# New cost figures for the planner that orders background work in a hybrid conv/SSM decoder step

## The chip, the cores and the metric

One NeuronCore of a Trainium2 chip. The time is device microseconds (us) of one execution, as the median of several; lower is better.

## What is computed

One layer for 2048 prompt tokens and 8 single-token samples, in fp32: a convolution branch and a state-space (SSM) branch from one input projection, each gated, an output projection, and a per-layer embedding step. Cut to what matters:

```python
h = rmsnorm(x, g_pre)
proj = h @ w_in                       # 1024 -> 6144 columns
u = c_a * sigmoid(c_b)
v, new_buf = causal_depthwise_conv(u, conv_buf, conv_w, conv_b)   # 31 taps
v = silu(layernorm(v, ln_g, ln_b)) * silu(c_z)
y_c = v @ w_pc
ys, sr, si = ssm_branch(s_x, ...)     # 32 groups, 64 complex states
ys = gelu(ys)
ys = ys * sigmoid(ys @ w_glu + b_glu) * silu(s_z)
y_s = ys @ w_ps
m = sigmoid(gc) * y_c + sigmoid(gs) * y_s
x = x + rmsnorm(m @ w_out, g_post)
e = rmsnorm(p @ w_ple, g_ple)
x = x + e * sigmoid(x @ w_pg + b_pg)
```

## The kernel before

**Tiles.** Channels lie on the 128 partitions, tokens along the free axis. The tokens are worked through in two halves: half 0 is 1024 prompt tokens and the 8 samples (blocks of 344 columns, three to a tile), half 1 the other 1024 (two blocks of 512). An fp32 product is made of three fp32r products on TensorE (PE): weight high part by activation high part (L288), high by low (L289), low by high (L290). ScalarE (ACT) makes the high part of a weight chunk, `whi` (L251), and GpSimd (POOL) the low part, `wlo` (L331, from `w_split`); there are four buffers of each. Activations have a high and a low part in the same way (`hh`/`hl`, `nh`/`nl`, `mh`/`ml`); the low part is a subtraction on VectorE (DVE) or POOL.

**Foreground.** `stages()` takes one weight chunk, issues for each block 3·k matmuls into one of the PSUM banks, adds their cost to the planner's PE clock (L293), lets the planner place background work (`bg.pump()`), and then writes the instruction that takes the result out of the bank. `stage_pair` (cost at L310) does the same for two chunks at once.

**Background.** Everything else is a task of the class `Background`: a Python generator that yields (engine, time from which it may run) and then writes one or a few instructions. `pump` compares the planner's own clocks of DVE (V), ACT (S) and POOL (G) with its PE clock and writes a task's next step into the program when it would start before PE's present time. So nothing is scheduled on the chip: the planner's costs `cV`, `cS`, `cG`, `cP4` (L138 to L142) and the PE cost decide where in each engine's in-order stream a step stands. `pick` (L90) decides between DVE and POOL for a subtraction or an addition. `drain` writes a task's remaining steps at once when the foreground needs them, and `room(n)` holds a task until n SBUF units are free.

The tasks that are named below:
- `ssm_setup`: a chain of small DVE operations on `spar` and `ph` tiles that ends in the tiles `gw` and `gt`; the first use by PE is a transpose of `gt` (L609).
- `rms_task`: sums of squares, `rt` on ACT (L984) and `re<-re,rt` on DVE.
- `conv_task`: the 31 taps of one channel tile, each one DVE operation `acc<-u,prm,acc` (L183). If enough units are free, `conv_side` takes two of the taps at a time from the other end with ACT (`cq`, L881) and POOL (`ca`), and `u<-acc,ca` joins the two sums on DVE.
- `ln_task` and `mean_task`: the layer norm of the conv output. The two means over the channels are PE products with a constant matrix (`nh` and `nl` by `avgr`, L363 and L364), each followed by ACT and DVE work. The first is called the mean product here, the second the norm product; each occurs once in either half.
- `gelu_task` (L1151) and `ysn_task` (L1206): the SSM output's activation and its split. `x1_task`: the residual after `w_out` (`o`, `xr`, then `mh` and `ml`). `y_task`: the last step (`e`, `sgp`).

A DVE step that evacuates or multiplies out a PSUM bank (`gs<-bank,gs`, `u<-bank,sg`) stands in the same in-order stream as the taps.

Of the kernel before, what the change touches and what calls it, by code (L numbers as in the profile page):

```python
# [21 lines left out]
G = 32  # L22
# [5 lines left out]
class Background:  # L28
# [61 lines left out]
    def pick(self, n, ready):  # L90

        v, g = (max(self.clock[e], ready) for e in "VG")
        return "V" if v + n / 960.0 <= g + n / 478.0 + 0.3 else "G"

    def use(self, e, cost, ready=0.0):

# [11 lines left out]
class Units:  # L108
# [8 lines left out]
    def alloc(self, dtype=F32, shape=None, name="un"):  # L117
        assert self.free_list, "no unit is free: " + " ".join(sorted(t.name for _, t in self.slot.values()))
        i = self.free_list.popleft()
        self.least = min(self.least, len(self.free_list))  # L120
        t = self.pool.tile([P, UW], dtype, tag=f"u{i}", name=f"{name}_{i}")
        self.slot[id(t)] = (i, t)
        return t
# [4 lines left out]
    def free(self, *ts):  # L128
        for t in ts:
            i, _ = self.slot.pop(id(t))  # L130
            self.free_list.append(i)


def build(nc, tc, A, O):
    V, S, T, GP, SY = nc.vector, nc.scalar, nc.tensor, nc.gpsimd, nc.sync
    bg = Background()
    use, fore = bg.use, bg.fore
    cV = lambda n: 0.08 + n / 960.0  # L138
    cV2 = lambda n: 0.08 + n / 1920.0
    cS = lambda n: 0.13 + n / 1250.0  # L140
    cG = lambda n: 0.16 + n / 478.0
    cP4 = lambda n: 4 * max(n, 128) / 2400.0  # L142
    queue = {"issue": 0.0, "data": 0.0}

# [13 lines left out]
    with ExitStack() as ctx:  # L158
# [12 lines left out]
        def bank():  # L171
            return ps_pool.tile([P, 512], F32, tag="bank", name="bank")
# [17 lines left out]
        def room(k):  # L190
            while units.left() < k:
                yield None, bg.now + 0.5
# [88 lines left out]
        def stages(key, todo):  # L281
            wt, k = take(key)
            for i, (m, rhs, evac, c0, n) in enumerate(todo):
                w = slice(m * P, m * P + P)
                o = bank()[:, 0:n]
                for kt in range(k):
                    (hi, lo), (rh, rl) = wt[kt], rhs[kt]
                    T.matmul(o, hi[:, w], rh[:, c0:c0 + n], start=kt == 0, stop=False)  # L288
                    T.matmul(o, hi[:, w], rl[:, c0:c0 + n], start=False, stop=False)  # L289
                    T.matmul(o, lo[:, w], rh[:, c0:c0 + n], start=False, stop=kt == k - 1)  # L290
                if i == 4 and wstate["split"] == wstate["use"]:
                    w_ahead(wstate["use"] - 1)
                bg.pe += 3 * k * (n / 2400.0 + 0.003)  # L293
                bg.pump()
                evac(m, o, c0, n)

        def stage_pair(keys, rhs, blocks, evacs):

            wts = [take(key, 0)[0] for key in keys]
            pts = [[bank()[:, 0:n] for _, n in blocks] for _ in keys]  # L300
            for kt, (rh, rl) in enumerate(rhs):
                e = kt == len(rhs) - 1
                for wt, os_ in zip(wts, pts):
                    hi, lo = wt[kt]
                    for o, (c0, n) in zip(os_, blocks):
                        T.matmul(o, hi, rh[:, c0:c0 + n], start=kt == 0, stop=False)
                        T.matmul(o, hi, rl[:, c0:c0 + n], start=False, stop=False)
                        T.matmul(o, lo, rh[:, c0:c0 + n], start=False, stop=e)  # L308
            w_ahead(wstate["use"], 0)
            bg.pe += 6 * len(rhs) * sum(n / 2400.0 + 0.003 for _, n in blocks)  # L310
            bg.pump(pe=False)
            for os_, evac in zip(pts, evacs):
                for o, (c0, n) in zip(os_, blocks):
                    evac(0, o, c0, n)
# [29 lines left out]
        def hilo(name):  # L344
            return alloc(F32R, name=name + "h"), alloc(F32R, name=name + "l")
# [733 lines left out]
        def half(h, hT, finish):  # L1079
            n, blocks = TOK[h], BLOCKS[h]  # L1080
# [68 lines left out]
            zs, ysg = [None] * NB, [None] * NB  # L1149

            def gelu_task(b):  # L1151
                yield "S", ready[b]
                zs[b] = alloc(name="z")
                S.activation(out=zs[b][:, 0:HT].rearrange("p (s q) -> p q s", q=8),
                             in_=ysb[b][:, 0:HT].rearrange("p (q s) -> p q s", q=8), func=AF.Gelu_apprx_tanh)
                if h == 0:
                    S.activation(out=zs[b][:, HT:n], in_=ysb[b][:, HT:n], func=AF.Gelu_apprx_tanh)
                free(ysb[b])
                r = use("S", cS(n) + 1.4, ready[b])
                yield from room(2)  # L1160
                ysg[b] = hilo("y")
                yield from split_task(zs[b], ysg[b], full, "G", r)
# [41 lines left out]
            free(sgl)  # L1204

            def ysn_task(b):  # L1206
                yield "S", ready[b]
                ysn[b] = hilo("yn")
                yield from split_task(zs[b], ysn[b], full, "A", ready[b])
                free(zs[b])  # L1210
# [375 lines left out]
```

## Time and profile before

| | |
|---|---|
| runs | 1972.57, 1973.45, 1979.47 us; median 1973.45 |
| profiled execution | 1971.99 us, span of its instructions 1970.2 us |
| PE busy | 1918.5 us (97%), 10386 matmuls |
| DVE busy | 1442.1 us (73%), 1696 instructions |
| ACT busy | 765.6 us (39%), 1276 instructions |
| POOL busy | 784.8 us (40%), 573 instructions |
| mean granted PE clock | 0.989 of full |

A share of busy time is a mean over the whole program. PE's busy time counts a matmul from its start to its modelled end, so matmuls that follow each other overlap; how fast PE goes is read from how many start in a stretch. A number in square brackets behind a row of a timeline is the time in which the engine stood idle before it, with what ended that time.

### The profile page before, as it was taken

What the parts mean: (1) busy time and instruction counts of PE and PEld (TensorE: products, weight loads), DVE (VectorE), ACT (ScalarE), POOL (GpSimd) and SP (SyncE); (2) the same over time, 40 slices, a digit from 0 to 9 for tenths busy, and PEclk for the clock granted to TensorE, in tenths of its full rate; (3) what the DMA queues carried; (4) which work ended last, traced back from release to release, by engine and by line L of the source; (5) the groups of instructions that cost most, each with busy time, mean ns of one, the idle gap of its engine ahead of it and who ended that gap; (6) DMA issues with size and microseconds to landing.
All of it is one profiled execution on the core that took longest, in us unless ns stands there. A gap on an engine that the chain in (4) does not pass through costs nothing.

```text
span 1970.2 us, 26641 instructions
## 1 busy us (share of the span) xinstructions
PE 1918.5 (97%) x10386; PEld 1723.0 (87%) x10386; DVE 1442.1 (73%) x1696; ACT 765.6 (39%) x1276; POOL 784.8 (40%) x573
## 2 busy tenths in 40 slices
PE   8897999999999999999899999999999999999998
PEld 7797999999999999999798788888888888888877
DVE  6889997899899876444884479888589843442686
ACT  7424211227311364254532223444731353223542
POOL 1437623315422223253533222687743222224554
PEclk9998999999999999999899999999999999999999
DMA  8461344542122215342554463212212211422455
GB/s 315 155 203 62 100 133 141 177 144 78 51 83 78 102 50 193 116 142 93 190 197 164 172 200 123 74 60 91 71 48 75 97 67 43 160 107 77 148 189 174
DMA packets 103286, 243.58 MB, mean 124 GB/s; under 512 B 11752, under 2 KB 44648, under 8 KB 103144
## 3 DMA queue, kind: packets, MB, share of 16 engines
q1 hardware_dynamic: 102840, 241.68, 36.2%
q8 instruction: 81, 1.33, 0.3%
q14 instruction: 45, 0.37, 0.1%
q10 hardware_dynamic: 320, 0.20, 0.0%
HBM read 188.17 MB, written 54.62 MB: 123 GB/s over the span
## 4 chain that ended last, share of the span: by engine, by line
PE 85%; issue 4%; DVE 4%; POOL 2%; ACT 1%; DMA 1%; POOLq 0%; ACTq 0%; SPq 0%; DVEq 0%
PE bank L288 27%; PE bank L290 26%; PE bank L289 26%; PE bank L774 2%; POOL wlo L331 1%; PE bank L777 1%; PE bank L719 1%; DMA raw<-in_w 1%; POOL ca L331 1%; DVE sgp L331 1%; DVE o L183 0%; DVE o L331 0%; DVE ml L331 0%; DVE spar L183 0%; PE bank L308 0%
## 5 line engine op out<-in xcount | busy, mean ns | idle before, releaser
L331 POOL TENSOR_TENSOR wlo<-raw,whi 128x512 fp32r<-128x512 f32 x386 | 566.5, 1486 | 1082.2 <-ACT whi L251 1064.5
L288 PE MATMUL bank<-hh,whi 128*128 128x344 f32 (+1 forms) x1888 | 665.9, 353 | 0.9 <-ACT whi L251 0.9
L289 PE MATMUL bank<-hl,whi 128*128 128x344 f32 (+1 forms) x1888 | 659.9, 350 | 6.8 <-DVE hl L331 6.8
L290 PE MATMUL bank<-hh,wlo 128*128 128x344 f32 (+1 forms) x1888 | 661.2, 350 | 1.4 <-POOL wlo L331 1.4
L183 DVE SCALAR_TENSOR_TENSOR acc<-u,prm,acc 128x1024 f32<-128x1024 f32 x412 | 530.5, 1288 | 11.2
L289 PEld LDWEIGHTS bank<-hl,whi 128*128 128x128 f32 x1888 | 356.9, 189 | 39.4 <-DVE hl L331 7.1
L288 PEld LDWEIGHTS bank<-hh,whi 128*128 128x128 f32 x1888 | 356.4, 189 | 36.9 <-ACT whi L251 1.5
L290 PEld LDWEIGHTS bank<-hh,wlo 128*128 128x128 f32 x1888 | 356.8, 189 | 35.6 <-POOL wlo L331 2.4
L251 ACT CAST whi<-raw 128x512 fp32r<-128x512 f32 x388 | 223.9, 619 | 148.5 <-PE bank L289 68.6
L288 PE MATMUL bank<-mh,whi 128*128 128x344 f32 (+1 forms) x640 | 227.4, 355 | 7.7 <-ACT whi L251 5.8
L290 PE MATMUL bank<-mh,wlo 128*128 128x344 f32 (+1 forms) x640 | 227.1, 355 | 5.2 <-POOL wlo L331 5.1
L289 PE MATMUL bank<-ml,whi 128*128 128x344 f32 (+1 forms) x640 | 226.6, 354 | 0.3 <-DVE ml L331 0.3
L331 POOL TENSOR_TENSOR ca<-ca,cq 128x512 f32<-128x512 f32 x104 | 132.2, 1300 | 39.5 <-ACT cq L881 36.1
L288 PEld LDWEIGHTS bank<-mh,whi 128*128 128x128 f32 x640 | 122.6, 192 | 20.8 <-ACT whi L251 7.1
L290 PEld LDWEIGHTS bank<-mh,wlo 128*128 128x128 f32 x640 | 122.7, 192 | 18.9 <-POOL wlo L331 7.8
L289 PEld LDWEIGHTS bank<-ml,whi 128*128 128x128 f32 x640 | 122.5, 191 | 12.3 <-DVE ml L331 1.1
L289 PE MATMUL bank<-vl,whi 128*128 128x344 f32 (+1 forms) x320 | 111.9, 350 | 0.7 <-DVE vl L331 0.7
L288 PE MATMUL bank<-vh,whi 128*128 128x344 f32 (+1 forms) x320 | 112.2, 351 | 0.0
L290 PE MATMUL bank<-vh,wlo 128*128 128x344 f32 (+1 forms) x320 | 112.0, 350 | 0.0
L881 ACT ACTIVATE cq<-u,prm 128x512 f32<-128x512 f32 x104 | 73.4, 722 | 55.0 <-POOL ca L331 45.9
L331 DVE TENSOR_TENSOR oacc<-oacc,sq 128x344 f32<-128x344 f32 (+1 forms) x35 | 30.6, 874 | 79.2 <-ACT sq L1388 78.7
L177 DVE TENSOR_TENSOR gcl<-bank,gcl 128x344 f32<-128x344 f32 (+1 forms) x40 | 23.5, 587 | 65.7 <-PE bank L290 65.7
(213 smaller groups left out, 2447.7 us busy)
## 6 DMA issues: line engine op xcount, KB each, us to landing
raw<-in_w SPq DMA_DIRECT2D x194, 512.0 KB
cq<-cq SPq DMA_DIRECT2D x12, 512.0 KB
e<-e SPq DMA_DIRECT2D x8, 516.0 KB
rt<-e SPq DMA_DIRECT2D x8, 516.0 KB
gc<-gc SPq DMA_DIRECT2D x8, 516.0 KB
m<-gs SPq DMA_DIRECT2D x8, 516.0 KB
gcl<-gc SPq DMA_DIRECT2D x8, 516.0 KB
m2l<-m SPq DMA_DIRECT2D x8, 516.0 KB
```

The lines of the kernel that those rows point to most:

```text
L177: V.tensor_tensor(out=out, in0=a, in1=b, op=op)
L183: V.scalar_tensor_tensor(out=out, in0=a, scalar=s, in1=b, op0=op0, op1=op1)
L251: S.copy(out=hi, in_=t[:, c])
L288: T.matmul(o, hi[:, w], rh[:, c0:c0 + n], start=kt == 0, stop=False)
L289: T.matmul(o, hi[:, w], rl[:, c0:c0 + n], start=False, stop=False)
L290: T.matmul(o, lo[:, w], rh[:, c0:c0 + n], start=False, stop=kt == k - 1)
L331: (V if e == "V" else GP).tensor_tensor(out=out, in0=a, in1=b, op=op)
L719: T.matmul(pvs[rr][half_[i], jj], we[:, g * P + rr * 64:g * P + rr * 64 + 64], U[:, g, 8:8 + ne], start=True, stop=True)
L774: T.matmul(pvs[i][:, jj], TW[:, :, 2 * j + i], U[:, 2 * j + i, o0:136], start=True, stop=False)
L777: T.matmul(pvs[i][:, jj], cq[half_[i], x * 512 + j * P:x * 512 + (j + 1) * P], X[half_[i], x, j, o0:136], start=False, stop=x == 1)
L881: S.activation(out=q[:, h], in_=u[:, k + x * 512:k + x * 512 + 512], func=AF.Identity, scale=w(k))
```

## The change

The planner's costs are replaced by other numbers, with a function of its own for a product (`cPr`), and two tasks wait for free SBUF units before and after their first yield.

```diff
     def pick(self, n, ready):
         v, g = (max(self.clock[e], ready) for e in "VG")
-        return "V" if v + n / 960.0 <= g + n / 478.0 + 0.3 else "G"
+        return "V" if v + n / 930.0 <= g + n / 478.0 + 0.4 else "G"
...
-    cV = lambda n: 0.08 + n / 960.0
+    cV = lambda n: 0.1 + n / 930.0
     cV2 = lambda n: 0.08 + n / 1920.0
-    cS = lambda n: 0.13 + n / 1250.0
-    cG = lambda n: 0.16 + n / 478.0
+    cS = lambda n: 0.13 + n / 1190.0
+    cG = lambda n: 0.3 + n / 478.0
+    cPr = lambda n: 0.007 + n * 0.4375e-3
...
-                bg.pe += 3 * k * (n / 2400.0 + 0.003)
+                bg.pe += 3 * k * cPr(n)
...
-            bg.pe += 6 * len(rhs) * sum(n / 2400.0 + 0.003 for _, n in blocks)
+            bg.pe += 6 * len(rhs) * sum(cPr(n) for _, n in blocks)
...
             def gelu_task(b):
+                yield from room(1)
                 yield "S", ready[b]
+                yield from room(1)
...
             def ysn_task(b):
+                yield from room(2)
                 yield "S", ready[b]
+                yield from room(2)
```

The work is the same; its order on the engines is not. The instructions of PE are the same in number, those of the background products stand elsewhere among the others. DVE has 410 instead of 412 taps `acc<-u,prm,acc`, and one `hl<-xT,hh` more, which POOL had. ACT has 44 instead of 38 table loads, and 108 instead of 104 `cq`; POOL 108 instead of 104 `ca`.

**DVE up to the mean product of half 0.** `u_3341` and `u_3323` are the last channel tile of the convolution, `gs<-bank,gs` takes a result of `w_ps` out of PSUM, and `nl` is the low part that the mean product needs. Before:

```order
L177 TENSOR_TENSOR gs_6114<-bank,gs_6114 128x344
L183 SCALAR_TENSOR_TENSOR acc<-u_3341,prm,acc 128x1024 x5
L183 SCALAR_TENSOR_TENSOR u_3341<-u_3341,prm,acc 128x1024
L1271 COPY u_3341<-vsm 128x8
L331 TENSOR_TENSOR acc_5266<-u_3341,acc_5266 128x1032
L331 TENSOR_TENSOR nl_6512<-acc_5266,nh_6511 128x1032
```

Now:

```order
L178 TENSOR_TENSOR gs_5822<-bank,gs_5822 128x344
L184 SCALAR_TENSOR_TENSOR acc<-u_3323,prm,acc 128x1024 x12
L184 SCALAR_TENSOR_TENSOR u_3323<-u_3323,prm,acc 128x1024
L1276 COPY u_3323<-vsm 128x8
L332 TENSOR_TENSOR acc_5276<-u_3323,acc_5276 128x1032
L332 TENSOR_TENSOR nl_6295<-acc_5276,nh_6294 128x1032
L178 TENSOR_TENSOR gs_6128<-bank,gs_6128 128x344 x2
```

The six evacuations `gs_6113` and `gs_6114` of before, now `gs_6128` and `gs_6129`, have moved behind `nl`. On PE the mean product stands 180 matmuls earlier. At the last evacuation ahead of these six (`gs_5809` before, `gs_5822` now) DVE has 207 taps behind it, where it had 192.

**DVE in the SSM setup.** `bb`, `spar` and `rho` are the setup's chain, `re<-re,rt` is a step of a norm that waits for `rt` of ACT. Before:

```order
L177 TENSOR_TENSOR bb_729<-bb_729 128x256
L331 TENSOR_TENSOR re_743<-re_743,rt_989 128x1032
L331 TENSOR_TENSOR re_743<-re_743,rt_1102 128x1032
L177 TENSOR_TENSOR spar_727<-spar_727 128x16 x2
L177 TENSOR_TENSOR rho<-spar_727 128x16
```

Now:

```order
L178 TENSOR_TENSOR bb_732<-bb_732 128x256
L332 TENSOR_TENSOR re_741<-re_741,rt_1026 128x1032
L178 TENSOR_TENSOR spar_730<-spar_730 128x16 x2
L178 TENSOR_TENSOR rho<-spar_730 128x16
L560 COPY spar_730<-spar_730 128x16
```

The second of the two norm steps has moved behind the next 25 rows of the chain; on ACT its `rt`, and the one ahead of it, have moved behind a pair of `whi`. Further on, a norm step that stood ahead of the first `gt` has moved behind it, and two taps have moved ahead of it.

**ACT behind the norm product of half 1.** `mean` and `acc` are the end of the norm, `u<-u,prm` its activation on the channel tiles, `gs` the evacuation of a gate with another activation function. Before:

```order
L383 ACT_TABLE_LOAD
L383 ACTIVATE mean_13883<-mean_13882 128x1024
L384 ACTIVATE acc_13159<-mean_13883 128x1024
L322 ACT_TABLE_LOAD
L322 ACTIVATE gs_13766<-bank 128x512
L251 CAST whi<-raw 128x512 x2
L1248 ACT_TABLE_LOAD
L1248 ACTIVATE u_10431<-u_10431,prm 128x1024
L1248 ACTIVATE u_10642<-u_10642,prm 128x1024
```

Now:

```order
L323 ACT_TABLE_LOAD
L323 ACTIVATE gs_13588<-bank 128x512
L252 CAST whi<-raw 128x512 x2
L1253 ACT_TABLE_LOAD
L1253 ACTIVATE u_10431<-u_10431,prm 128x1024
L323 ACT_TABLE_LOAD
L323 ACTIVATE gs_13589<-bank 128x512
L1253 ACT_TABLE_LOAD
L1253 ACTIVATE u_10642<-u_10642,prm 128x1024
```

The norm product has moved 192 matmuls ahead on PE, so its activations now alternate with gate evacuations, each change of function with a table load.

## Rows read from the trace of the kernel before

**Rows 1.** The page's chain of work that ended last: shares of the span.

```profile
PE 85%; issue 4%; DVE 4%; POOL 2%; ACT 1%; DMA 1%; POOLq 0%; ACTq 0%; SPq 0%; DVEq 0%
```

**Rows 2.** Windows: us, busy (x starts) of PE, PEld, DVE, ACT, POOL; clock; DMA.

```profile
500.00:550.00 50.00, 50.00 (x319) 50.00 (x318) 43.28 (x47) 19.93 (x34) 20.66 (x13) 1.00 0.16 45
1500.00:1600.00 100.00, 100.00 (x432) 80.96 (x431) 76.93 (x69) 36.37 (x50) 25.45 (x18) 1.00 0.23 78
```

**Rows 3.** Waits of PE over the span: us in total, times, longest.

```profile
PE bank L609 <- issue: 14.1, 1, 14.1
...
PE bank L289 <- DVE hl L331: 6.8, 1, 6.8
...
PE bank L289 <- DVE psl L331: 0.2, 1, 0.2
```

**Rows 4.** Timeline of PE behind the first transposes of gt: start, us, instruction.

```profile
196.91 0.64 PE L288 MATMUL bank<-hh,whi 128*128 128x344 f32 x1
...
202.07 0.31 PE L288 MATMUL bank<-hh,whi 128*128 128x344 f32 x1
```

**Rows 5.** Timelines of DVE and ACT in the SSM setup.

```profile
104.06 1.23 DVE L331 TENSOR_TENSOR re<-re,rt 128x1032 f32<-128x1032 f32 x1 [5.18 <-ACT rt L984]
...
99.22 1.15 ACT L251 CAST whi<-raw 128x512 fp32r<-128x512 f32 x2
```

**Rows 6.** Timelines of DVE and POOL ahead of the last hl.

```profile
72.69 6.85 DVE L183 SCALAR_TENSOR_TENSOR spar<-spar 128x16 f32<-128x16 f32 x6
...
81.54 1.22 DVE L183 SCALAR_TENSOR_TENSOR spar<-spar 128x16 f32<-128x16 f32 x6
...
83.17 0.87 DVE L331 TENSOR_TENSOR hl<-xT,hh 128x688 fp32r<-128x688 f32 x1
...
75.37 1.70 POOL L331 TENSOR_TENSOR hl<-xT,hh 128x688 fp32r<-128x688 f32 x1
```

**Rows 7.** Costliest groups: one tap; us busy, mean ns of one.

```profile
L183 DVE SCALAR_TENSOR_TENSOR acc<-u,prm,acc 128x1024 f32<-128x1024 f32 x412 | 530.5, 1288 | 11.2
```

**Rows 8.** Waits of DVE from 196 to 626 us, first and last of ten.

```profile
DVE u L177 <- PE bank L290: 10.4, 6, 3.0
...
DVE gs L177 <- PE bank L290: 4.8, 9, 1.6
...
DVE gs L177 <- issue: 0.2, 1, 0.2
```

**Rows 9.** Timelines of DVE and PE at the layer norm of half 0.

```profile
626.25 14.52 DVE L183 SCALAR_TENSOR_TENSOR acc<-u,prm,acc 128x1024 f32<-128x1024 f32 x11
...
672.82 2.21 DVE L331 TENSOR_TENSOR nl<-acc,nh 128x1032 fp32r<-128x1032 f32 x1 [4.05 <-ACT nh L338]
...
704.17 1.23 DVE L331 TENSOR_TENSOR nl<-acc,nh 128x1032 fp32r<-128x1032 f32 x1 [1.12 <-ACT nh L338]
...
677.76 0.32 PE L363 MATMUL bank<-nh,avgr 128*128 128x344 f32 x1
```

**Rows 10.** The stage w_pg of half 0: a window, and DVE's timeline in it.

```profile
936.00:990.00 54.00, 43.17 (x224) 39.79 (x224) 43.61 (x42) 26.97 (x43) 29.15 (x18) 0.85 0.57 194
...
974.16 1.60 DVE L331 TENSOR_TENSOR sgp<-sgp,e 128x344 f32<-128x344 f32 x1
975.79 0.52 DVE L331 TENSOR_TENSOR sgp<-sgp,o 128x344 f32<-128x344 f32 x1
```

**Rows 11.** Timeline of DVE in half 1, up to the mean product.

```profile
1434.41 1.22 DVE L177 TENSOR_TENSOR u<-acc,ca 128x1024 f32<-128x1024 f32 x1 [27.86 <-POOL ca L331]
...
1547.21 1.23 DVE L331 TENSOR_TENSOR nl<-acc,nh 128x1024 fp32r<-128x1024 f32 x1 [1.11 <-ACT nh L338]
```

**Rows 12.** Timelines of PE and ACT at the norm product of half 1.

```profile
1552.45 0.39 PE L363 MATMUL bank<-nh,avgr 128*128 128x512 f32 x1
...
1588.75 1.28 ACT L383 ACT_TABLE_LOAD   x1
1590.04 1.07 ACT L383 ACTIVATE mean<-mean 128x1024 f32<-128x1024 f32 x1
```

## Prediction, made before the changed kernel ran

> **What bounds the kernel now.** I read the chain of waits first: 85% of the span is PE, and no other engine has more than 4% [rows 1]. PE's pace comes next, from the windows: undisturbed it starts 319 matmuls of 344 columns in 50 us, 157 ns each, and 432 of 512 columns in 100 us, 231.5 ns each, at full clock [rows 2]. The planner used to reckon 146 and 216 ns (n/2400 + 0.003); now it reckons 157.5 and 231. So the new product cost is what the rows show. But the planner's clock runs nothing on the chip. It only sets the order, and the order matters only where PE waits. Third, therefore, PE's own waits: eleven kinds, the longest 14.1 us at the first transpose of `gt`, then 6.8 us for `hl` of DVE, the last 0.2 us [rows 3]. What a wait costs beyond itself is in PE's timeline behind the 14.1 us: from 196.91 to 202.07 there are 18 matmul steps, 287 ns each where full clock gives 157, so 18 x 0.13 = 2.3 us more at the lower clock level [rows 4]. The third lossy place is the stage `w_pg` of half 0: in 54 us only 224 matmuls start, which at 157 ns are 35.2 us; 18.8 us are lost at a granted clock of 0.85 [rows 10]. These three places lose about 14.1 + 2.3 + 6.8 + 18.8 = 42 us of 1972. A gain has to come from there. Everywhere else the change can only keep PE fed or stop feeding it.
>
> **The change part by part.** The matmuls are the same, so each part is a question whether its DVE, ACT or POOL step is late for PE.
>
> *The last `hl` of the input norm (PE waits 6.8 us for it).* It still stands behind the same chain of small `spar` operations. One more `hl` goes through DVE (0.87 us) and none through POOL (1.70 us) [rows 6]. The same six small operations took 6.85 us beside POOL and 1.22 us without [rows 6]. If the chain gets faster by the POOL operation's whole length, the wait changes by 0.87 - 1.70 = -0.8; if not at all, by +0.9. I take 0.
>
> *`gt` (PE waits 14.1 us).* The row names no engine, but `gt` is the end of DVE's setup chain, and PE starts as soon as it is there; so what is added to this chain is added to PE's wait. DVE idled 5.18 us for `rt` until 104.06 [rows 5]. Now only the first of the two norm steps stands there, and its `rt` follows the `whi` pair that ends at 99.22 + 1.15 = 100.4 [rows 5]; with about 1.1 us for itself it is done at 101.6, and the norm step at 102.8, against 105.3: -2.5. The second step comes later (+1.2), a later one leaves for behind `gt` (-1.2), two taps come in (2 x 1.29 = +2.6 [rows 7]). The sum is +0.1. Against it, the chain's small operations now run where the old wait lay, beside POOL; six at the price of rows 6 (1.14 instead of 0.20 us) would be +5.6, none would be 0. I take +1, nearer to none since only some 3 us of the old wait are refilled; bounds -2 and +5.
>
> *The mean product of half 0.* This is the largest term that is open. The product stands 180 matmuls earlier: 677.76 - 180 x 0.157 = 649.5 [rows 2, 9]. Its `nl` ended at 672.82 + 2.21 = 675.0 [rows 9]. After the last `gs` evacuation before it, behind which the next taps started at 626.25, DVE now has 12 taps (15.8 us at 14.52/11 = 1.32 [rows 9]), the last tap and two joins (2.9), the wait for `nh` (about 1.2) and `nl` (2.2): 22.1 us, so 648.4 if DVE has no backlog at 626.25. That is 1 us to spare. The backlog is the question: up to that evacuation 15 more taps are placed than before, two of them ahead of `gt`, where PE waits along with DVE. The other 13 are 13 x 1.32 = 17.2 us. Up to 626 us DVE's ten kinds of waits sum to 30.8 us, 10.4 + 4.8 = 15.2 of them for PE's banks [rows 8]; there the stream had nothing else to do, and these the earlier taps fill. 17.2 - 15.2 leaves 2 us, less the 1 to spare: +1. Bounds 0 (all absorbed) and 17.2 - 1 = 16 (none).
>
> *The norm product of half 0* stands 186 matmuls behind the mean product instead of 198: 29.2 us. From the mean product to the end of `nl` the chain took 704.17 + 1.23 - 677.76 = 27.6 us [rows 9]. Six evacuations now lie in it, a norm step has left. Each evacuation adds about 0.6, the step was 2.3, so 28.9 against 29.2, with the matmul itself to finish first: +1, bounds 0 and +3.
>
> *`w_pg` of half 0* is a chain on DVE (43.6 of 54 us busy [rows 10]). Before its last `ml`, now five pairs of `sgp` operations stand instead of four, two operations more of 0.52 to 1.60 us [rows 10]; that is +1.0 to +3.2, I take +2. The `mh` of ACT stand in another order among the `whi`; what that gives I bound by a third of the 18.8 us lost, 6, in favour.
>
> *Half 1.* The mean product moves 168 matmuls ahead: 1552.45 - 168 x 0.2315 = 1513.6 [rows 2, 12]. `nl` ended at 1548.4, 35 us later [rows 11]. What pays for it: the 27.86 us that DVE waited for POOL's `ca` until 1434.4 [rows 11] now hold taps of another tile, four evacuations of 0.6 leave, and one tile has two taps fewer on DVE; 27.9 + 2.4 + 2.6 = 32.9, and a start of the last tile without backlog gives the rest. I take 0, bounds 0 and +4. The four `cq` and `ca` more lie on ACT and POOL, which have room.
>
> *Six more table loads* stand behind half 1's norm product, now among gate evacuations. One takes 1.28 us, and the operation behind it starts 10 ns after it ends (1588.75 + 1.28, then 1590.04) [rows 12]. From the norm product to the weight chunk after next PE has 120 matmuls, 27.8 us [rows 2]. ACT's stream has in it six loads (7.7 us) and 15 operations, by my estimate 12 us; with the wait for DVE's first `u` and POOL's `wlo` behind, some 25 us. So 0, with 3 us of room.
> A rule of the Trainium skill speaks against this part: "ScalarE: Activation LUTs", section "What ACT_TABLE_LOAD costs", states 1283 ns for a load and about 1380 ns of drain with each switch. The first agrees with the row, the second does not: no gap of that size stands behind this load. By the page six switches would be 8.3 us longer, PE would wait some 5 us, and the sum would be 1982; by the row it stays.
>
> The remaining moves (small SSM products by 3 to 18 us, the norm of x by 77 us, earlier) come where DVE has slack; I cost them at nothing. If that cover were gone, each is bounded by one tap ahead of it, 1.3 us.
>
> Sum: 0 + 1 + 1 + 1 + 2 + 0 + 0 = +5 on the profiled execution's 1971.99, thus **1977.0**. The median of the runs is 1973.45, 1.5 above the profiled one; against it the forecast is +3.5. About 0.5%, 9.9 us, is what a measurement of this kernel tells from no change: under 1963.6 is faster, over 1983.3 slower.
>
> **The rivals.**
> *DVE late for the mean product (slower).* The taps that moved forward don't fit into DVE's waits, because those lie between bank evacuations too short to take a tap, and `nl` of half 0 becomes PE's wait. For it: DVE is busy 43 of 50 us at 500 [rows 2], and just 1 us is to spare. Against it: the waits total 30.8 us. Price with nothing absorbed: 16 instead of 1, and the lower clock behind it 2.3: 1977 + 15 + 2.3 = 1994. It decides from a backlog of 7 us on (1977 + 6.3 = 1983.3).
> *The chains get shorter (faster).* `gt` comes 2 us earlier, `hl` 0.8, and `w_pg` gives back 6 instead of costing 2: 1977 - 3 - 0.8 - 8 - 1 for the clock behind them = 1964; with another 2 us where PE waits for `whi` it is 1962. For it: the 5.18 us wait does go. Against it: the two taps and the extra `sgp` operations stand ahead of what PE waits for.
> *Nothing that counts moves.* The change reorders covered work alone, and the terms of +1 and +2 cancel: 1972, within 3 us.
>
> **How the numbers follow.** Forecast (a small loss, 1974 to 1983): 0.45. Nothing moves: 0.16. DVE late: 0.22, of it 0.20 beyond 1983.3. Chains shorter: 0.17, of it 0.15 below 1963.6. Loss terms that add up (`gt` +5, `w_pg` +3, half 1 +4) take another 0.03 of the forecast's share over the bound. So faster 0.15, slower 0.23, same 0.62. The range is 1962 to 1992: it takes in the faster rival's value and most of the late DVE's. The likeliest case's own range is 1971 to 1983.
>
> **What would show it.** In the new profile `gt` should start within 3 us of 196 and PE wait 13 to 18 us at its transpose; the mean product of half 0 should start at 649 to 653 with DVE's waits from 196 to 626 down by over 12 us. `w_pg` should still lose 17 to 23 us. Behind half 1's norm product the 512-column matmuls should keep 231.5 ns. The forecast is wrong if PE waits over 7 us for `nl`, or if `gt` or `w_pg` come more than 6 us earlier.

## The result and the profile after

The changed kernel is slower: 2005.49 us (median of 4 runs, 2004.40 to 2007.02) against 1973.01 for the kernel before on the same chip; the ratio is 1.0158, 95% interval 1.0135 to 1.0180. The forecast was 1977.0 with a range up to 1992. The profiled execution took 2004.40 us, 32.4 more than that of before.

The chain of waits in the page of the changed kernel, which answers to [rows 1]:

```profile
PE 79%; DVE 7%; issue 7%; POOL 3%; DMA 3%; ACT 2%; SPq 1%; POOLq 0%; ACTq 0%; DVEq 0%
```

PE still sets the end, but its share has gone from 85 to 79%, and DMA has risen from 1 to 3%. The waits of PE over the span (us in total, times, longest), against [rows 3]:

```profile
PE bank L289 <- ACT whi L252: 12.8, 5, 6.9
PE bank L289 <- ACT mh L339: 10.7, 2, 5.6
PE bank L610 <- issue: 10.1, 1, 10.1
PE bank L720 <- DMA swe<-we: 8.6, 1, 8.6
...
PE bank L610 <- DVE gt L178: 5.4, 1, 5.4
PE bank L289 <- DVE u L178: 4.9, 1, 4.9
...
PE bank L365 <- DVE nl L332: 2.6, 2, 2.0
...
PE bank L290 <- DVE hl L332: 1.7, 1, 1.7
```

The old wait at the first `gt` is 10.1 instead of 14.1, that for `hl` 1.7 instead of 6.8. The total for `whi` is nearly the same (13.1 before). New are a wait for `swe`, a second one for `gt`, one for `u`, two for `nl`, and 10.7 for `mh` (1.9 before).

The foreground's 9600 matmuls (those with `whi` or `wlo`) stand in the same order in both kernels. So the difference in the start of the n-th, in the two profiled executions, is a running account. Near the start it is good to some 3 us only: five of the kernels below have the order of the kernel before up to the 1020th matmul, and they start the 330th 0.9 to 3.0 us later than it and the 1020th 0.3 to 2.6.

| n-th | start before | start after | late by | lost in between |
|---|---|---|---|---|
| 330 | 73.2 | 80.0 | +6.8 | +6.8: the start |
| 400 | 93.6 | 93.0 | -0.6 | -7.4: the wait for `hl` is shorter |
| 1020 | 210.9 | 212.1 | +1.1 | +1.7: first `gt` |
| 1700 | 342.9 | 343.5 | +0.6 | -0.5 |
| 2150 | 436.2 | 455.0 | +18.8 | **+18.2: the SSM products** |
| 5300 | 939.6 | 959.0 | +19.4 | +0.6: the whole conv and layer norm of half 0 |
| 5600 | 1008.1 | 1033.0 | +24.9 | **+5.5: `w_pg` of half 0** |
| 7600 | 1494.9 | 1520.7 | +25.8 | +0.9 |
| 7900 | 1565.4 | 1596.7 | +31.2 | **+5.4: norm of half 1** (0.9 of it four matmuls that moved in) |
| 9599 | 1964.7 | 1997.2 | +32.4 | +1.2 |

**The SSM products.** One window from 340 to 440 us of each kernel (columns as in [rows 2]), of before:

```profile
340.00:440.00 100.00, 99.97 (x679) 96.07 (x678) 91.66 (x102) 24.62 (x61) 24.83 (x19) 1.00 0.47 162
```

and now:

```profile
340.00:440.00 100.00, 86.00 (x562) 82.29 (x561) 86.14 (x94) 19.38 (x51) 24.69 (x18) 0.91 0.42 149
```

117 matmuls fewer start, 18.4 us at 157 ns. DVE's timeline of the changed kernel has a long wait here:

```profile
341.56 1.28 DVE L184 SCALAR_TENSOR_TENSOR acc<-u,prm,acc 128x1024 f32<-128x1024 f32 x1
352.65 0.17 DVE L707 COPY sc<-sfin 128x8 f32<-128x8 f32 x1 [9.80 <-DMA cq<-cq]
...
353.01 3.36 DVE L178 TENSOR_TENSOR gw<-pwr,bb 128x512 f32<-128x512 f32 x2
356.40 0.69 DVE L178 TENSOR_TENSOR gt<-gw 128x512 f32<-128x512 f32 x1
```

For a copy of 0.17 us DVE is idle for 9.80 us, until a DMA that reads `cq` is done. The copy doesn't read `cq`; its output `sc` has been given the SBUF unit of `cq`. `alloc` takes the unit that has been free longest (L117 to L131), and in the order of this kernel that is the one which `ssm_setup` had freed right behind its store of `cq`; the store was still reading it. Behind the copy stand `gw` and `gt`, for which PE waits 5.43 us. In the kernel before the order was the other way round:

```profile
342.08 1.29 DVE L177 TENSOR_TENSOR gw<-pwr,bb 128x512 f32<-128x512 f32 x2
343.40 0.69 DVE L177 TENSOR_TENSOR gt<-gw 128x512 f32<-128x512 f32 x1
...
355.21 0.74 DVE L706 COPY sc<-sfin 128x8 f32<-128x8 f32 x1
```

Further on the same thing happens on POOL. The next `cq` has been given the unit of `kd`, freed in the line ahead of it, so it has to wait until DVE has written `kd` (374.53) and the eight `tt` transfers have read it. SP issues its DMAs in order, so the load of `swe` stands behind the transfer of this `cq`; it also has the unit of this `cq`, and the runs don't tell the two apart. POOL, SP and PE:

```profile
380.92 1.29 POOL L646 TENSOR_TENSOR cq<-gw 128x512 f32<-128x512 f32 x1 [19.51 <-DMA tt<-kd]
...
387.71 0.34 SPq L154 DMA_DIRECT2D cq<-cq  x1
...
391.62 0.32 SPq L154 DMA_DIRECT2D swe<-we  x1
...
396.31 1.59 PE L720 MATMUL bank<-U,swe 128*64 128x136 f32 x11 [8.57 <-DMA swe<-we]
```

Before, SP issued `cq` at 375.73 and `swe` at 376.24, and the products with `swe` stood 24 matmuls further back in PE's order. The waits are 5.43 + 8.57 = 14.0 us. Of the other 4, about 3 are matmul steps of 287 ns behind the two waits, at the lower clock level (0.91 in the window, as in [rows 4]).

**`w_pg` of half 0.** The same foreground matmuls as in the window of [rows 10] now lie from 955.5 to 1015.4, 59.9 us instead of 54:

```profile
955.50:1015.40 59.90, 41.65 (x224) 38.60 (x223) 46.00 (x47) 26.83 (x43) 28.89 (x18) 0.82 0.54 179
```

DVE's timeline shows five `sgp` pairs ahead of the last `ml` (these are three of them), and then a wait for the residual's load `xr`:

```profile
994.58 1.60 DVE L332 TENSOR_TENSOR sgp<-sgp,e 128x344 f32<-128x344 f32 x1
996.21 1.49 DVE L332 TENSOR_TENSOR sgp<-sgp,o 128x344 f32<-128x344 f32 x1
...
999.45 0.51 DVE L332 TENSOR_TENSOR sgp<-sgp,e 128x344 f32<-128x344 f32 x1
999.99 0.52 DVE L332 TENSOR_TENSOR sgp<-sgp,o 128x344 f32<-128x344 f32 x1
1000.43 0.51 DVE L332 TENSOR_TENSOR sgp<-sgp,e 128x344 f32<-128x344 f32 x1
1000.97 0.52 DVE L332 TENSOR_TENSOR sgp<-sgp,o 128x344 f32<-128x344 f32 x1
1001.40 0.87 DVE L332 TENSOR_TENSOR o<-o,xr 128x688 f32<-128x688 f32 x1
...
1003.04 1.94 DVE L332 TENSOR_TENSOR o<-o,xr 128x688 f32<-128x688 f32 x1
...
1011.18 0.88 DVE L332 TENSOR_TENSOR o<-o,xr 128x688 f32<-128x688 f32 x1 [3.56 <-DMA xr<-in_xT]
```

PE waits for `mh` twice:

```profile
1003.82 0.66 PE L289 MATMUL bank<-mh,whi 128*128 128x344 f32 x1 [5.64 <-ACT mh L339]
...
1012.91 0.66 PE L289 MATMUL bank<-mh,whi 128*128 128x344 f32 x1 [5.07 <-ACT mh L339]
```

In the kernel before, DVE waits for no `xr` at this place; the last add follows the `sgp` pair ahead of it at once:

```profile
984.48 1.48 DVE L331 TENSOR_TENSOR sgp<-sgp,o 128x344 f32<-128x344 f32 x1
985.88 0.86 DVE L331 TENSOR_TENSOR o<-o,xr 128x688 f32<-128x688 f32 x1
```

**The norms.** The mean product of half 0 starts at 669.71 without a wait, `nl` having started at 667.55; 669.7 less the 20 us by which everything is late here is 649.3. In half 1, DVE and PE at the norm product:

```profile
1569.85 1.23 DVE L332 TENSOR_TENSOR nl<-acc,nh 128x1024 fp32r<-128x1024 f32 x1 [2.99 <-DMA m<-gs]
...
1571.13 0.80 PE L365 MATMUL bank<-nl,avgr 128*128 128x512 f32 x1 [2.02 <-DVE nl L332]
...
1572.57 0.63 PE L289 MATMUL bank<-hh,whi 128*128 128x512 f32 x1
1573.00 0.63 PE L290 MATMUL bank<-hl,whi 128*128 128x512 f32 x1
```

`nl` reads neither `m` nor `gs`; it has been given a unit that `gs` had, and waits for the DMA that still reads it, the third case of this kind. Behind it PE steps at 427 ns per matmul of 512 columns instead of 231.5, until 1574.28 us.

### The profile page after: what moved, and what is told of

It is laid out like the page before. It is cut to its first block, busy times and chain, and to the rows that moved or that the text cites. A ratio compares the mean times of both kernels' runs of the same rounds, so it can differ in the third digit from the quotient of the medians.

```text
span 2002.6 us, 26647 instructions
## 1 busy us (share of the span) xinstructions
PE 1924.2 (96%) x10386; PEld 1726.9 (86%) x10386; DVE 1438.9 (72%) x1695; ACT 775.8 (39%) x1287; POOL 790.1 (39%) x576
## 4 chain that ended last, share of the span: by engine, by line
PE 79%; DVE 7%; issue 7%; POOL 3%; DMA 3%; ACT 2%; SPq 1%; POOLq 0%; ACTq 0%; DVEq 0%
PE bank L289 25%; PE bank L290 24%; PE bank L291 24%; POOL wlo L332 2%; PE bank L775 2%; PE bank L778 1%; DMA raw<-in_w 1%; DVE ph L178 1%; PE bank L720 1%; DVE acc L184 1%; SPq L154 1%; DVE acc L332 1%; DVE spar L181 1%; DVE o L332 0%; DMA cq<-cq 0%
## 5 line engine op out<-in xcount | busy, mean ns | idle before, releaser
L289 PE MATMUL bank<-mh,whi 128*128 128x344 f32 (+1 forms) x640 | 227.8, 356 | 15.5 <-ACT mh L339 10.7
L332 POOL TENSOR_TENSOR ca<-ca,cq 128x512 f32<-128x512 f32 x108 | 137.4, 1303 | 26.1 <-ACT cq L882 26.1
L289 PEld LDWEIGHTS bank<-mh,whi 128*128 128x128 f32 x640 | 122.4, 191 | 28.5 <-ACT mh L339 11.4
L332 DVE TENSOR_TENSOR cz<-cz,u 128x1032 f32<-128x1032 f32 (+1 forms) x16 | 20.6, 1295 | 79.8 <-ACT cz L323 79.8
```

The source lines that it names most:

```text
L332: (V if e == "V" else GP).tensor_tensor(out=out, in0=a, in1=b, op=op)
```

## The experiments

**Is it the units? Runs e1_late, e5_unit, e2_late_before.** In the first, the two copies into `sc` are moved in the program behind the next yield, to where `sc` is first needed:

```diff
             yield "V", 0.0
-            V.tensor_copy(out=X[:, :, :, 8], in_=sfin[:, :, js])
-            if first:
-                V.tensor_copy(out=X[:, :, :, 0:8], in_=s0[:, :, js, :])
             use("V", 0.3)
...
             yield "V", r
+            V.tensor_copy(out=X[:, :, :, 8], in_=sfin[:, :, js])
+            if first:
+                V.tensor_copy(out=X[:, :, :, 0:8], in_=s0[:, :, js, :])
             turn(E, E, False)
```

> The changed kernel, with the planner's decisions untouched but the two small copies into the state tile of each SSM batch written just ahead of the rotation that needs them, so that on DVE they stand behind the last gw and gt. Theory 1 (the copy waits 9.8 us for a DMA that still reads its unit, and everything behind it in DVE's stream is late): the two PE waits of 5.4 us (transposes of the last gt) and 8.6 us (swe) go, with 3 to 5 us of slow clock; 2005.5 becomes 1985 to 1990. Theory 2 (the SSM products were moved too far ahead on PE and would wait for gt and swe anyway): 2001 to 2006.

Measured: 1994.10 us, ratio to before 1.0099 [1.0084, 1.0114]; 11.4 us less than the changed kernel, between the two theories. The wait for the second `gt` is gone. That for `swe` is half as long:

```profile
384.82 1.59 PE L717 MATMUL bank<-U,swe 128*64 128x136 f32 x11 [3.98 <-DMA swe<-we]
```

So the copy's wait is the larger part of the SSM loss, not all of it. e5_unit adds to e1's edit one swap, by which `cq` is given the unit of `we` instead of that of `kd`:

```diff
-                free(kdu, we)
+                free(we, kdu)
                 cq = alloc(name="cq")
```

> The first experiment with one more line: the units of we and kd are given back in the other order, so that POOL's cq tile takes the unit that one DMA reads and not the one that eight read. Theory 1 (what is left in the SSM stretch, the 4.0 us wait for swe, is the same thing once more: POOL waits 11 us for DMAs that still read its unit, its DMA holds SP's queue, and swe stands behind it): the wait falls to under 1.5 us and 1994 becomes 1988 to 1991. Theory 2 (the swe product stands 32 matmuls too early on PE for any order of the loads): the wait stays at 3 to 4 us, 1993 to 1995.

Measured: 1987.27 us, 1.0071 [1.0056, 1.0086]; 6.8 less than e1. PE waits for no `swe` any more, and its window is back at the pace of before:

```profile
340.00:440.00 100.00, 100.00 (x681) 96.48 (x680) 97.42 (x111) 23.70 (x60) 26.63 (x21) 1.00 0.52 179
```

POOL's wait ahead of this `cq` is 4.48 us, where it was 11.11 in e1. The two edits change neither the work nor a cost, only which unit is written when. Together they give back 18.2 us by the medians; by the account the place, which lost 18.2, gains 0.4. So this loss is shown to hang on the two units and on what stands behind them. That the copy waits for its unit is read from its row and from `alloc`: no run gives the copy another unit in the same order. e2_late_before makes e1's edit in the kernel before.

> The same move in the kernel before. There the copies wait 5.2 us at 372.8 and nothing on PE waits for what stands behind them. Theory 1: 1973 within 2 us. If deferring these copies is worth something by itself (theory 3), 1965 to 1969.

Measured: 1972.02 us, 0.9992 [0.9982, 1.0001]. There the copies stood behind `gt`. One of them waited 5.2 us for POOL, which was reading a unit that `sc` got; e2 takes this wait away and gains nothing measurable; PE had no wait there to lose.

**`w_pg`: the loads of the residual. Runs e3_xr, e6_all, e12_after_x4.** A tile of `x1_task` may begin its load when the third tile before it is done; e3_xr lets it begin one tile earlier.

```diff
             def x1_tile(k, c, cc, m, got):
-                while c > 2 and not x1s[k][c - 3][3]:
+                while c > 3 and not x1s[k][c - 4][3]:
```

> The changed kernel, with a residual tile (xr) loaded when the fourth-last tile is done instead of the third-last. Theory 1 (the last xr load stands on SP's queue behind a weight load that waits for its buffer, so the last two residual adds come late): the 3.6 us wait for xr in w_pg of half 0 goes and the time falls by 3 to 6 us to 1999.5 to 2002.5. Theory 2 (the residual chain is bound by DVE's own work, with two more sgp pairs in it): within 2 us of 2005.5.

Measured: 1996.77 us, 1.0117 [1.0098, 1.0137], 8.7 less than the changed kernel. But the edit also moved DVE's order: two `sgp` pairs instead of five now stand ahead of the last `ml`. So it shows what the place is worth, not whether load or order did it. e6_all has the edits of e5 and e3 together.

> The changed kernel with the three corrections together (copies late, units swapped, xr loaded one tile earlier). Theory 1 (three separate collisions, at 340 to 400 us and at 1000 us, make up most of the loss): the gains add up, 2005.5 - 11.4 - 4 to 6 - 8.7 = 1980 to 1982. Theory 2 (a wait that goes comes back elsewhere): over 1986.

Measured: 1979.34 us (10 runs), 1.0031 [1.0021, 1.0040]. The gains add: 26.2 of 32.5 us are found again. Not all of that is loss undone: at `w_pg`, which lost 5.5 us, the edit gives 10.3 by the account. With one more tile of lead (`c > 4`, `c - 5`) nothing is gained:

> The sixth experiment with xr loaded two tiles earlier than in the changed kernel. If loads still come late in w_pg of half 0: 2 to 6 us less than the sixth, 1973 to 1977. If the chain there is DVE's own work by now: within 2 us of the sixth's 1979.

Measured: 1982.07 us, 1.0042 [1.0028, 1.0056].

**Load or order? Runs e9_no_xr, e13_no_xr, e14_no_y, e17_no_y_no_xr.** e9 leaves the residual's load out of the sum in one tile:

```diff
-                r = ew(e, o[:, cc], o[:, cc], t[:, 0:m], ALU.add, m, r)
+                r = ew(e, o[:, cc], o[:, cc], o[:, cc] if (h, k, c) == (0, 1, 7) else t[:, 0:m], ALU.add, m, r)
```

> The changed kernel, where the last residual add of half 0 (the later part, channel tile 7) adds its tile to itself instead of the loaded xr; that one tile's residual is left out. Every engine's order is that of the changed kernel, one wait is gone. Theory 1 (the late load is what w_pg lost over before): the 3.6 us wait goes with 1 to 2 us of slow clock, 2005.5 becomes 2000 to 2001.5. Theory 2 (the five pairs of sgp operations ahead of the last ml set the end of the chain, the load is hidden behind them): 2004 to 2006.

Measured: 2004.93 us, 1.0161 [1.0147, 1.0175]. Another tile had the wait (it stayed, at 3.17 us), so this tells nothing. e13 does it for tiles 4 to 7 (`h == 0 and k == 1 and c > 3`).

> The changed kernel, where the residual adds of half 0's later part on channel tiles 4 to 7 add the tile to itself instead of the loaded xr (those residuals are left out); the order on every engine is the changed kernel's. Theory 1 (the late loads cost w_pg its 5.5 us): the 3.6 us wait goes and 2005 becomes 2000 to 2001.5. Theory 2 (the sgp operations ahead of the last ml do): 2003.5 to 2006.

Measured: 2003.31 us, 1.0146 [1.0129, 1.0163]; by the account (5300th to 5600th) 3.4 us of the place are back: the second `mh` wait falls from 5.1 to 1.4, the first stays (5.5). e14 takes out DVE's `y_task` operations of part 0 in half 0 instead:

```diff
-                stt(e[:, 0:m], e[:, 0:m], vcol("g_ple", c), re_[:, cc], ALU.mult, ALU.mult)
+                if h or k:
+                    stt(e[:, 0:m], e[:, 0:m], vcol("g_ple", c), re_[:, cc], ALU.mult, ALU.mult)
```

(and likewise the two `sgp` operations).

> The changed kernel without the 24 DVE operations of y_task on the earlier part of half 0 (that part of the output is left out); the order of all else, and the loads, as they are. Theory 2 (these operations hold the residual chain): w_pg's chain falls by what stands ahead of the last ml, five groups of e and two sgp of 0.5 to 1.6 us each, 10 to 14 us in all, so 1993 to 1997 if the chain is the limit to its end, and before's w_pg and the changed one's come out alike in e14 and e15 within 2 us. Theory 1 (late loads): 2002 to 2005, the wait for xr grows.

Measured: 2000.74 us, 1.0136 [1.0121, 1.0151]; 5.0 us back by the account. The first `mh` wait falls from 5.6 to 1.9. The second grows to 7.6; DVE waits 4.66 us for `xr` ahead of it. e17 has both edits.

> The changed kernel with both of the last experiments' edits in it: half 0's y operations of part 0 (24 of VectorE, that output left out) are not run, and the residual adds of tiles 4 to 7 of part 1 take the tile itself in place of the residual's load (residual left out). The place loses some 5.5 us against the program before; each edit alone gave 3.6 us there. Theory 1 (VectorE's queue and the residual's loads are two bounds of nearly the same length, so that either one alone keeps most of the wait): together they give back more than the sum of the two, 8 to 11 us at the place, and no wait of TensorE for mh over 1.5 us is left; 1994 to 1998. Theory 2 (the edits are two ways to the same wait, VectorE's queue alone): together they give no more than 5 us, 1999 to 2002, and a wait for mh of some 2 us stays. Theory 3 (the loss there is in the sum of VectorE's work of part 1 alone): as theory 2, and the wait that stays is for VectorE's o with VectorE busy ahead of it.

Measured: 1998.79 us, 1.0129 [1.0108, 1.0151]. PE's waits there, where the changed kernel had 10.7:

```profile
PE bank L289 <- ACT mh L339: 4.1, 2, 2.6
```

By the account 9.1 us are back, against 3.4 + 5.0 = 8.4 for the two edits alone; by the medians it is 6.7 against 2.2 + 4.8. The kernels with the changed order at this place (the changed one, e1, e5 and e9) lose 4.3 to 5.5 us there, so 0.7 is no clear excess: the gains add, and the first theory, by which either bound hides what the other gives, is not borne out in the sum. What is shown is that the first `mh` wait goes with DVE's `y` operations and the second with the loads, and that the second takes back 2.5 us of what the first gives (e14). The wait that is left is longer than the first theory said.

**The same places in the kernel before. Runs e10_before_xr, e11_before_all, e15_no_y_before, e18_before_hold.** e3's edit in it:

> The kernel before with xr loaded one tile earlier (the edit of the third experiment). Before loses 18.8 us in w_pg of half 0. Theory 1 (the residual chain there is held by late loads and by y_task's operations among it): 5 to 9 us less, 1964 to 1968. Theory 2 (before's loads came in time, the chain is bound by DVE's own operations): 1971 to 1974.

Measured: 1984.93 us, 1.0060 [1.0048, 1.0073]; all theories wrong. PE waits 11.98 us for one `mh` at 998.76, since the last tile's add moved behind six `sgp` pairs in a row and then waits 2.80 us for its `xr`. A correction that gave 8 us in one order costs 12 in the other. All three edits:

> The kernel before with all three corrections (copies late, units swapped, xr earlier). Theory 1: as the tenth experiment, within 2 us, since the first two correct collisions that before does not have. If they do help there: 2 to 4 us less than the tenth.

Measured: 1984.44 us, 1.0059 [1.0045, 1.0072]; as e10, so the two SSM edits are worth nothing where nothing waits. e14's edit in the kernel before:

> The same in the kernel before (four groups ahead of the last ml). Theory 2: 1964 to 1967, w_pg of half 0 loses 9 to 12 us instead of 18.8. Theory 1: 1971 to 1973.

Measured: 1967.37 us, 0.9969 [0.9958, 0.9980]; 6.5 us at the place by the account. So part of the loss of [rows 10] is DVE's `y` operations. But they cost about as much in the changed kernel (5.0 in e14). Without them the two kernels don't come out alike at this place, as e14's second theory asked: they are 7.0 us apart, where they were 5.5. So the extra `sgp` pair alone did not make the difference; the late loads, which only the changed kernel has, are the larger part of it (3.4 of 5.5 in e13). e18 keeps the `y` operations and holds them back:

```diff
+                if k == 0 and h == 0 and c > 2:
+                    while len(x1s[1]) < NT or not all(t[3] for t in x1s[1]):
+                        yield None, bg.now + 0.5
```

> The kernel before, with the y operations of tiles 3 to 7 of part 0 in half 0 held back until all x1 tiles of part 1 are done. Taking the 24 y operations out of the kernel before gave 1967.4 (-5.6). Theory 1 (they cost time only because they stand ahead of part 1's adds in VectorE's queue): held back they give most of that, 1966 to 1970. Theory 2 (held back they only move: their operands keep their units longer, the store of the output and the loads behind it come late, or they meet w_pg's later groups): 1972 to 1980, with a wait of TensorE or SyncE's queue between 1000 and 1100 us that the kernel before doesn't show.

Measured: 1977.68 us, 1.0015 [1.0004, 1.0026]. Up to 963 us PE is 4.6 us earlier, at 995 it is 5.3 later: the adds now come in time, but the last ones wait for `o` and its loads, and PE waits for `mh` three times.

```profile
PE bank L288 <- ACT mh L338: 10.8, 3, 6.4
```

A further 3.4 us go by the 6000th matmul, most of it at 1058, where PE waits 3.19 us for `whi` (1.73 in the kernel before). Held back, the operations only move the loss.

**Which of the new costs does it? Runs e4_cv_only, e7_cv200, e8_cv200_all, e16_taps.** The waits for room and the number in `pick` change no engine's order. Of the new costs, DVE's is put in alone (with room). With the product cost or POOL's alone the planner finds no free unit; ACT's alone was not run.

```diff
-    cV = lambda n: 0.08 + n / 960.0
+    cV = lambda n: 0.1 + n / 930.0
```

> The kernel before with the new VectorE cost alone (and the room lines, which move nothing). Theory 1 (what the change costs hangs on a few collisions of in-order streams, not on the rates being right or wrong): its time differs from before by the collisions of its own order, anywhere between 1970 and 2000, and each difference from before of more than 2 us has one PE wait behind it. Theory 2 (a higher DVE cost makes the plan too slack or too tight everywhere): many small PE waits, no single one over 2 us that before has not.

Measured: 1987.89 us, 1.0068 [1.0051, 1.0085]. PE's waits for the first `gt` and for `hl` are gone, and PE is 18.1 us earlier at the 1020th foreground matmul. Then it loses 9 us between the 1700th and the 2150th, in the SSM products, and 26 between the 4000th and the 4300th, at the start of the stage `w_pc`. So DVE's cost by itself makes a slower order, with its loss at another place than the changed kernel's; that any one cost is behind the changed kernel's loss is not shown. e7 applies the new DVE cost only while the planner's PE clock is under 200 us.

> The kernel before with the new VectorE cost only while the planner's PE clock is under 200 us, and the old costs behind it. With that cost alone for the whole program DVE reached gt before PE did and the 14 us wait was gone. Theory 1 (the gain is local to the order up to gt, and the cost's losses further on were other collisions): 1954 to 1960. Theory 2 (what is taken out of the stretch up to gt has to be done behind it and makes PE wait there): 1968 to 1974.

Measured: 1984.62 us, 1.0065 [1.0048, 1.0082]. Against the kernel before it is 19.6 us ahead at the 1020th foreground matmul (191.3 us), 10.6 ahead at the 4000th (720.8), and 12.4 behind at the 4300th (792.2). PE's waits in between are these:

```profile
PE bank L288 <- ACT vh L338: 8.0, 5, 2.6
PE bank L289 <- DVE vl L331: 5.4, 5, 1.7
```

Both come out of the layer norm, on DVE. Its `nl` of the mean product starts at 692.97; in the kernel before it was 672.82 [rows 9], though the last evacuation ahead of it came later there. That evacuation in the kernel before, then in e7, with e7's `nl`:

```profile
659.09 0.52 DVE L177 TENSOR_TENSOR gs<-bank,gs 128x344 f32<-128x344 f32 x1 [0.19 <-PE bank L290]
```

```profile
648.80 0.52 DVE L177 TENSOR_TENSOR gs<-bank,gs 128x344 f32<-128x344 f32 x1 [0.17 <-PE bank L290]
...
692.97 1.23 DVE L331 TENSOR_TENSOR nl<-acc,nh 128x1032 fp32r<-128x1032 f32 x1 [1.12 <-ACT nh L338]
```

Between the two DVE has 13.7 us in the kernel before and 44.2 in e7. So it is not only that PE arrives earlier: DVE comes to `nl` 20 us later, with more work placed ahead of it. e16 takes 16 of tile 6's taps in half 0 out of e7's kernel.

```diff
-                    stt(out if k == PAD else acc, u[:, k:k + HT], w(k), acc, ALU.mult, ALU.add)
+                    if not (h == 0 and c == 6 and 2 <= k < 18):
+                        stt(out if k == PAD else acc, u[:, k:k + HT], w(k), acc, ALU.mult, ALU.add)
```

> The seventh experiment (the new VectorE cost up to 200 us) with 16 taps of channel tile 6 in half 0 left out, 21 us of DVE work, order kept. Theory 1 (DVE's sum of work in half 0 bounds the layer norm, so time won at gt is lost at w_pc): the 20 us at w_pc go and 1984.6 becomes 1963 to 1967. Theory 2 (the order of the layer norm's last steps does it): 1982 to 1985.

Measured: 1984.63 us, 1.0058 [1.0043, 1.0073]; no change, and the same waits for `vh` and `vl`. From 605 to 650 us DVE then waits 18.5 us for `whi` of ACT, by way of a bank, and 7.2 for PE's banks: it has nothing to do there. What decides stands behind the last evacuation, here at 650.36: 23 taps and the steps of the next half's norm (`re`, `nl<-re`), 44 us with less than 2 us of idle time up to `nl`. e8 is e7 with e6's edits.

> The same with the three corrections of the sixth experiment. Theory 1: another 5 to 9 us less than the seventh experiment in w_pg of half 0 and nothing in the SSM stretch unless the seventh shows a wait there: 1946 to 1954. Theory 2: within 2 us of the seventh.

Measured: 1988.62 us, 1.0077 [1.0061, 1.0093]. By the account the SSM products get 8 us better than in e7, `w_pg` 10 us worse (one wait of 13.1 us for `mh`, as in e10). No version with all of the work is measurably faster than the kernel before; the best with the new costs is e6.

## Why the prediction was wrong

- **The step that failed** is the last one: the small SSM products that move by 3 to 18 us "come where DVE has slack; I cost them at nothing", each "bounded by one tap ahead of it, 1.3 us". The SSM stretch lost 18.2 us (e1 and e5 give them back). The bound counted only DVE's work ahead of the moved step. It did not ask whether the SBUF unit into which the step writes is still being read, nor what stands behind the step in the queues of DVE and SP. In the changed order `sc<-sfin` stands ahead of `gw` and `gt`, for which PE waits. The trace of before had a wait of this kind among the ten of [rows 8], 5.2 us for another such copy; the prediction has it only in the sum of 30.8:

```profile
DVE sc L706 <- POOL cq L645: 5.2, 1, 5.2
```

- **`w_pg`, +2 (+1.0 to +3.2, and up to 6 in favour).** The five pairs are there; it lost 5.5. Mis-sized: the term had only DVE's operations in it and no load. With the late loads out of the sum (e13) the place loses 2.1, near the forecast; that these 2.1 are the extra pair is not shown. The clock fell a little further (0.82 against 0.85). "Should still lose 17 to 23 us" was 59.9 - 224 x 0.157 = 24.7.
- **The mean product of half 0, +1 (0 to 16).** Right: neither it nor the norm product of half 0 (+1) has a wait, and with that the rival "DVE late" is wrong. DVE's waits for PE's banks between the first `gt` and 626 us fell from 15.2 to 5.0 us, so the earlier taps did go into them. The forecast that all of DVE's waits there fall by over 12 us failed by the letter (30.8 to 24.8), because the new 9.80 is one of them.
- **`gt`, +1.** +1.7 by the account, within what executions of one order differ by; PE's transpose starts at 197.84, within 3 us of 196. The place was right, its form was not: 4.86 us are now lost at 182.32 for `u` and 10.1 at the transpose, where 13 to 18 were forecast.
- **`hl`, 0.** -0.6 by the account, but as +6.8 up to the 330th matmul and -7.4 behind it, where the wait for `hl` fell from 6.8 to 1.7. The term was right by luck, through two errors. Of the +6.8, 2.4 are a wait of a background product for `acc` of DVE at 46.58 us; up to 3 can be the difference between executions; the rest is open.
- **Half 1, 0 (0 to +4).** 5.4 - 0.9 = 4.5 us, a little over its bound, but not where it was looked for: the mean product waits 0.55 us, the rest is lost at the norm product, by the unit that `m<-gs` reads and the clock behind it. "Should keep 231.5 ns" was wrong for the first five matmuls behind it (four of 427 ns, one of 364). That this is the unit is read from the row and was not tried by itself; e6 still has the wait (1.9 us).
- **Six table loads, 0.** Right: the only wait at this place (1571.13) is ahead of them, and from 1572 to 1660 us PE has none. A load at 1573.52 takes 1.28 us, and the activation behind it starts at 1574.81. So the drain that the Trainium skill, "ScalarE: Activation LUTs", section "What ACT_TABLE_LOAD costs", states with each switch doesn't show here either, and the sum by it, 1982 with a wait of PE, was not borne out.

Against the profiled execution the sum missed by 27.4 us (32.4 instead of 5): 18.2 in the SSM stretch, 3.5 in `w_pg`, 4.5 in half 1, the rest in small terms. The range failed because none of its rivals was of this kind. Nor did the signs that it named come up: PE waits at most 2.0 us for `nl`, and neither `gt` nor `w_pg` comes 6 us earlier.

## What to carry to other kernels

When buffers come from a shared list, a step that is moved ahead can inherit a buffer that a transfer still reads. Before costing it at nothing, ask whose buffer it gets and when that one's last DMA ends, and count everything that stands behind it in the engine's and the DMA queue's order. In a statically ordered program, better cost figures need not give a better order: what is gained at one place (18 us up to the 1020th matmul in e4) was more than lost at another (26 us in `w_pc`), where the same order put more DVE work ahead of what PE needs. And where two waits follow each other, take away both causes, singly and together: in e14 the second wait took back part of what the first gave.

## What the runs showed of the hardware

- The same DVE addition takes two times. `sgp<-sgp,e` of 344 columns takes 1.60 us at 994.58 and 0.51 at 999.45, `o<-o,xr` of 688 takes 0.87 at 1001.40 and 1.94 at 1003.04. POOL's `wlo` operations ran from 990.69 to 997.33 and from 1002.66 on:

```profile
990.69 6.64 POOL L332 TENSOR_TENSOR wlo<-raw,whi 128x512 fp32r<-128x512 f32 x4 [3.50 <-ACT whi L252]
1002.66 3.45 POOL L332 TENSOR_TENSOR wlo<-raw,whi 128x512 fp32r<-128x512 f32 x2 [5.33 <-ACT whi L252]
```

  The Trainium skill, "SBUF — State Buffer", section "Who interferes with whom", says that a DVE instruction with two SBUF inputs contends with a GpSimd instruction that reads SBUF; these rows agree. The taps, which read `u` and `acc` from SBUF, do not: of the changed kernel's 410, 149 lie for over nine tenths of their time beside a POOL addition or subtraction and take 1.288 us on average, and the 183 beside none take 1.287. For the additions no fixed figure per element can hold both times, so a planner with measured mean rates can still be wrong at a given place.
- A wait of PE costs more than itself: behind the 2.02 us for `nl` the 512-column matmuls stepped by 427 ns instead of 231.5, at a granted clock of 0.51 from 1571.1 to 1574.6, the lower of its two levels (1.2 GHz) for nearly all of it; that cost some 1.7 us more.
